# A hybrid trunk's mixer: large GpSimd operations moved to VectorE and ScalarE, and a chain's four output norms done at once

## The chip, the core and the metric

One core of a Trainium2 chip runs the whole program. The metric is the device time of one execution in microseconds; the value shown for a kernel is the median of its runs. Besides, one execution of each kernel is recorded by the hardware profiler. In its rows PE is TensorE (PEld its weight loads), DVE is VectorE, ACT is ScalarE, POOL is GpSimd and SP is SyncE, which issues the DMAs. L1124 is line 1124 of the kernel before.

## What is computed

A step of an encoder: 1024 prompt frames and 8 running streams of 16 frames (the "samples"), 1152 tokens of width 1024. A gated feed-forward (SwiGLU), a mixer, a second feed-forward, a final RMS norm. The mixer has two halves: four heads of a gated delta rule, and four groups of trailing means ("the pool half"). The delta rule of one head, cut from the reference:

```python
a_mat = jnp.where(strict, beta[..., :, None] * kk * decay, 0.0) + jnp.eye(chunk, dtype=f32)
sol = lax.linalg.triangular_solve(a_mat, rhs, left_side=True, lower=True, unit_diagonal=True)
u, w = sol[..., :dv], sol[..., dv:]
qk = jnp.einsum('bnhid,bnhjd->bnhij', q, k) * decay
def step(S, xs):
    q_c, qk_c, u_c, w_c, k_c, gl = xs
    v_new = u_c - jnp.einsum('bhcd,bhde->bhce', w_c, S)
    o_c = jnp.einsum('bhcd,bhde->bhce', q_c, S) + jnp.einsum('bhij,bhje->bhie', qk_c, v_new)
    S = S * jnp.exp(gl)[..., None, None] + jnp.einsum('bhcd,bhce->bhde', k_c, v_new)
    return S, o_c
...
o = rms_norm(o.astype(h.dtype), o_norm) * jax.nn.silu(gate.reshape(B, L, DN_HEADS, DN_HEAD_DIM))
```

Then the two halves are joined and multiplied with w_out. Everything is float32; the large products split each operand into a high and a low part and add three products.

## The kernel before

Tokens lie in the free dimension, channels in the partitions. The tokens come in three pieces: 512, 320 and 320. The program has three stages: the first feed-forward, the mixer, the second feed-forward. Only the mixer is touched.

The mixer runs over two blocks: block A has the first 512 tokens (four units of 128), block B has the other 512 prompt tokens and the 128 sample tokens. Per block and head there are tasks, written as Python generators: projections with a short convolution (letters p, v), the gate's projection (g), `prework` (w, and t for the samples), `inverse` (y and z), `chain` (c) or `chain_sample` (s), the pool half's means, mapping and split (m, n, x), and the product with w_out (o). The projections and the products with w_out, in a fixed list `fill`, are what keeps TensorE busy; the rest is urgent and small. A loop at the end writes the tasks into one program: it keeps a modelled time of TensorE, and where a generator yields a number it comes back to that task so many microseconds (times 1.35) later. The framework beneath then sets each engine's order from this program; an engine runs its own instructions strictly in that order. So an instruction that waits holds all that stands behind it on its engine.

What the change touches:

- `prework` computes decays, and from key products the matrix Vn (L1060), its pooled columns Vc (L1083, L1085), the query product AT (L1071). GpSimd scales the queries, q times U, in L1074, and raises a norm to a power in L1050.
- `inverse` solves the triangular system: GpSimd spreads Vc into Xs (L1096), TensorE multiplies it with a block matrix (the products of 384 columns, into `ps_b`), then fifteen small steps on VectorE (L1120, L1121), and L1124 places the blocks. GpSimd forms Gs, a masked Vn (L1131), for the merges that follow, which begin with transposes by TensorE (L62, into `ps_b`).
- `chain` steps through the four units of a head: a correction r, the new values vn (L1210), the new state (L1218), and the output `po`. `out_unit` norms it: ScalarE squares it with a sum (L1180) and copies it (L1181), VectorE scales the sum (L1182), GpSimd raises it to -1/2 (L1183), ScalarE multiplies (L1184). Its `finish` is a transpose by TensorE (L62, into `ps_c`) and VectorE's multiplication with the gate (L1190); it runs one unit later, for the last unit after a yield of 2.
- `chain_sample` does the same for the sample streams, each with a state of its own, S8: eight matrices of 128 columns. GpSimd masks vn eight times into `vz` (L1266) and scales S8 (L1268); two products of 512 columns are added to it by VectorE (L1275).
- `oz_split` splits a half's result into high and low for the product with w_out: ScalarE casts (L1008), and the low part is a subtraction (L1009) on GpSimd for the pool half, on VectorE for the other.

GpSimd also subtracts the low part of the weights of w_out (L186, 128x1024 each), and it copies small histories. VectorE evacuates the projections (L960, L963), runs the convolutions (L981, L987) and the pool half's means (L1323, L1329), and adds the outputs to x (L1002).

## Time and profile before

| | |
|---|---|
| median of 3 runs | 2192.55 us (2190.09 to 2193.48) |
| the profiled execution | 2195.53 us, its span 2193.7 us |
| TensorE busy | 2132.2 us, 97% of the span |
| VectorE, ScalarE, GpSimd busy | 1526.1, 917.5, 684.9 us |
| granted TensorE clock | 0.992 |
| chain of waits, by engine | PE 82%, DVE 10%, issue, DMA, POOL and ACT 2% each |

A row of a group of instructions reads: line, engine, operation, out<-in by the names of the buffers (their numbers left out), shape and count, then the busy time in microseconds, the mean of one in nanoseconds, and the idle time of the engine just before them with what ended it. A row of waits reads: who waited, for whom, microseconds in total, times, the longest. A row of the timeline: start, length, engine, line, operation, tiles, count, and in brackets the idle time before it. An idle engine off the bound costs nothing; what counts is where TensorE waits.

### The profile page before, as it was taken

Reading aid. Unit: us, or ns where it says so; the run is one execution under the profiler, and the core shown is the slowest. Engines: PE = TensorE matmul, PEld = TensorE weight load, DVE = VectorE, ACT = ScalarE, POOL = GpSimd, SP = SyncE. Lnnn points to the kernel's source line nnn. Section 1 sums busy time; section 2 is a strip of 40 time slices with the busy share of each in tenths; the row PEclk is TensorE's granted clock in tenths of the full one; section 3 lists DMA queues with packets and bytes.
Section 4 is the critical chain, followed back from the end, with each engine's and each line's share of the span. In section 5 each row is a group of like instructions: output and inputs, shape, how many; then the busy total and the mean of one; then the engine's idle time right before and its main releaser. Section 6 shows DMA issues by size and latency. Waiting matters only on the chain.

```text
span 2193.7 us, 33164 instructions
## 1 busy us (share of the span) xinstructions
PE 2132.2 (97%) x12341; PEld 1920.7 (88%) x12341; DVE 1526.1 (70%) x2736; ACT 917.5 (42%) x1854; POOL 684.9 (31%) x616
## 2 busy tenths in 40 slices
PE   9999999999999999999999998999999999999997
PEld 7899999998889887777989887889999999987997
DVE  7866666677347877778687867776666668743776
ACT  6433333444223455544444443543433335422333
POOL 1433333440014422322232333243333335100443
PEclk9999999999999999999999999999999999999998
DMA  6332333554556522111212123342333337446572
GB/s 252 120 124 103 128 109 112 183 202 147 184 195 218 179 86 61 57 61 59 94 55 80 44 93 93 134 145 92 127 110 123 115 129 248 142 125 225 198 256 74
DMA packets 102674, 289.72 MB, mean 132 GB/s; under 512 B 16240, under 2 KB 24304, under 8 KB 102256
## 3 DMA queue, kind: packets, MB, share of 16 engines
q1 hardware_dynamic: 101360, 286.40, 38.6%
q8 instruction: 97, 1.59, 0.3%
q10 hardware_dynamic: 1152, 1.19, 0.2%
q14 instruction: 65, 0.53, 0.1%
HBM read 214.89 MB, written 72.66 MB: 131 GB/s over the span
## 4 chain that ended last, share of the span: by engine, by line
PE 82%; DVE 10%; issue 2%; DMA 2%; POOL 2%; ACT 2%; DVEq 0%; SPq 0%; POOLq 0%; ACTq 0%
PE ps_a L58 31%; PE ps_b L58 20%; PE ps_d L58 17%; PE ps_c L58 14%; DVE O L288 2%; DVE B L981 1%; DVE O L186 1%; DVE A L1121 1%; PE ps_b L62 1%; DVE A L1323 1%; DMA x<-g_keep 1%; DVE x L654 1%; DMA R<-in_wd 1%; DVE A L1120 0%; POOL Q L282 0%
## 5 line engine op out<-in xcount | busy, mean ns | idle before, releaser
L58 PE MATMUL ps_a<-B,O 128*128 128x320 f32 x3040 | 509.1, 311 | 9.0 <-DVE x L654 5.8
L58 PEld LDWEIGHTS ps_a<-B,O 128*128 128x128 f32 x3040 | 465.7, 189 | 20.5 <-issue 8.6
L58 PE MATMUL ps_a<-A,O 128*128 128x320 f32 (+1 forms) x1952 | 426.3, 354 | 2.9 <-DVE A L1121 1.6
L58 PEld LDWEIGHTS ps_a<-A,O 128*128 128x128 f32 x1952 | 330.0, 190 | 37.6 <-issue 3.9
L288 DVE TENSOR_TENSOR O<-Q,O 128x512 fp32r<-128x512 f32 (+1 forms) x238 | 210.6, 886 | 193.6 <-ACT O L287 192.7
L58 PE MATMUL ps_b<-A,O 128*128 128x512 f32 (+1 forms) x1128 | 264.5, 388 | 5.2 <-ACT O L287 5.2
L58 PEld LDWEIGHTS ps_b<-A,O 128*128 128x128 f32 x1128 | 208.9, 189 | 45.8 <-ACT O L287 5.2
L58 PE MATMUL ps_d<-A,O 128*128 128x512 f32 x1056 | 244.2, 391 | 2.7 <-DVE x L606 1.8
L58 PEld LDWEIGHTS ps_d<-A,O 128*128 128x128 f32 x1056 | 196.8, 188 | 49.0 <-issue 4.0
L287 ACT CAST O<-Q 128x512 fp32r<-128x512 f32 (+1 forms) x238 | 143.2, 605 | 225.2 <-POOL Q L282 60.8
L288 DVE TENSOR_TENSOR O<-R,O 128x512 fp32r<-128x512 f32 (+1 forms) x216 | 197.7, 920 | 33.2 <-ACT O L287 32.4
L58 PE MATMUL ps_d<-B,O 128*128 128x320 f32 (+1 forms) x1104 | 206.1, 331 | 5.4 <-DVE x L1002 3.7
L282 POOL TENSOR_TENSOR Q<-R 128x512 f32<-128x512 f32 (+1 forms) x44 | 59.9, 1361 | 453.7 <-DMA R<-in_wd 279.0
L58 PE MATMUL ps_c<-A,O 128*128 128x512 f32 (+1 forms) x816 | 187.2, 377 | 0.8 <-DVE O L288 0.8
L58 PEld LDWEIGHTS ps_d<-B,O 128*128 128x128 f32 x1104 | 172.2, 189 | 16.1 <-DVE x L1002 5.9
L287 ACT CAST O<-R 128x512 fp32r<-128x512 f32 (+1 forms) x216 | 131.1, 611 | 126.5 <-PE ps_a L58 51.3
L58 PEld LDWEIGHTS ps_c<-A,O 128*128 128x128 f32 x816 | 145.6, 188 | 25.0 <-DVE O L288 1.3
L185 ACT CAST O<-R 128x1024 fp32r<-128x1024 f32 (+1 forms) x86 | 85.9, 1010 | 183.6 <-PE ps_d L58 133.7
L58 PE MATMUL ps_c<-B,O 128*128 128x320 f32 x912 | 144.6, 309 | 0.0
L58 PEld LDWEIGHTS ps_c<-B,O 128*128 128x128 f32 x912 | 136.8, 188 | 0.3
L393 POOL TENSOR_TENSOR A<-A,A 128x512 fp32r<-128x512 f32 x44 | 72.6, 1651 | 162.3 <-ACT A L392 162.2
L186 DVE TENSOR_TENSOR O<-R,O 128x1024 fp32r<-128x1024 f32 (+1 forms) x74 | 86.5, 1176 | 50.6 <-ACT O L185 29.7
(309 smaller groups left out, 3061.4 us busy)
## 6 DMA issues: line engine op xcount, KB each, us to landing
g_keep<-x SPq DMA_DIRECT2D x98, 320.0 KB, 2.5
R<-in_wg SPq DMA_DIRECT2D x48, 512.0 KB, 3.8
R<-in_wd SPq DMA_DIRECT2D x48, 512.0 KB, 3.7
R<-in_wu SPq DMA_DIRECT2D x47, 512.0 KB, 3.6
g_keep<-A SPq DMA_DIRECT2D x44, 512.0 KB, 2.6
A<-g_keep SPq DMA_DIRECT2D x44, 512.0 KB, 5.5
B<-g_keep SPq DMA_DIRECT2D x56, 320.0 KB, 6.3
A<-g_keep SPq DMA_DIRECT2D x42, 320.0 KB, 5.0
```

Of the source, the lines that this page charges most:

```text
L58: self.put(nc.tensor.matmul(out, lhs, rhs, **k), n / 2400 + .003 if lhs.dtype == F32R else max(n, lhs.shape[-1]) / 600)
L62: self.put(nc.tensor.transpose(out, lhs, rhs), out.shape[-1] / 1200)
L185: A.copy(hi, raw)
L186: (e or V).tensor_sub(lo, raw, hi.bitcast(F32))
L282: G.tensor_add(t, *src)
L287: Blocks.high = A.copy(hi, src).ins
L288: Blocks.mark = V.tensor_sub(lo, src, hi.bitcast(F32)).ins
L393: G.tensor_sub(go[:, 1], sg, go[:, 0].bitcast(F32))
L654: V.scalar_tensor_tensor(xk(c, d), ps, by, xk(c, d), ALU.mult, ALU.add)
L981: V.scalar_tensor_tensor(y[:, :512], raw[:, t:t + 512], cw[:, t:t + 1], y[:, :512], ALU.mult, ALU.add)
L1121: V.tensor_tensor(Uc[:, :, m + 1:], Uc[:, :, m + 1:], tu[:, :n, :w], ALU.add)
L1323: V.tensor_tensor(buf[:, :, :have], cur[:, :, w_:w_ + have], cur[:, :, :have], ALU.add)
```

## The change

The five larger GpSimd operations of `prework`, `inverse` and the pool half's split (L1074, both L1096, L1131, L1009 for the pool half) are issued on VectorE. In `chain_sample` the masked copies become eight ScalarE multiplications, and the scaling of S8 goes into VectorE's addition, which becomes eight operations that read one 128-column matrix, its scalar and the product in PSUM. `out_unit` is parted: `out_sums` squares and copies per unit, and `out_norm` does sum, power, four multiplications, four transposes into one PSUM tile and one multiplication with the gate, after the chain's last unit (yields 2.5 and 0.8, before 2 and 0.5). GpSimd keeps the powers and L186. The buffers for the sums hold four columns, the sample's output gets its own buffer, `osbs`.

```diff
--- before.py
+++ after.py
@@ -827,10 +827,10 @@
 
     ms.place(region("A4"), ("raw", WIDE, 2), ("ss", 32, 2), ("sss", 32, 2), ("ucar", 60, 1), ("cst", 288, 1))
     ms.place(region("A5"), ("Xs", 768, 1), ("DT", 512, 1), ("MV", 512, 1), ("DTs", P, 1), ("Vns", P, 1))
-    ms.place(region("A6"), ("z", WIDE, 1), ("Vc", 64, 1), ("Uc", 64, 1), ("tu", 64, 1), ("wpl", P, 1), ("sso", 1, 8), ("tt", 1, 8),
+    ms.place(region("A6"), ("z", WIDE, 1), ("Vc", 64, 1), ("Uc", 64, 1), ("tu", 64, 1), ("wpl", P, 1), ("sso", 4, 3), ("tt", 4, 3),
              ("half", 8, 1), ("small", 8, 1), ("nega", NH, 1), ("cout", 36, 1), ("Xss", 192, 1), ("Vc", 64, 1), ("vn", P, 2),
              ("sc", 120, 2), ("av", 80, 1), ("gm", 32, 1))
-    ms.place(region("R2"), ("eglS", 32, 1), ("scout", 288, 1), ("Vcs", 16, 2), ("Ucs", 16, 1), ("tus", 16, 1))
+    ms.place(region("R2"), ("eglS", 32, 1), ("osbs", P, 1), ("scout", 288, 1), ("Vcs", 16, 2), ("Ucs", 16, 1), ("tus", 16, 1))
     ms.place(region("R3"), ("big", 1024, 1))
     ms.place(region("B0"), ("k", 640, 1), ("q", 640, 1), ("gate", 640, 2))
     ms.place(region("B6"), ("k", 640, 1), ("q", 640, 1), ("kd", 512, 2), ("r", P, 1), ("rs", P, 1))
@@ -1071,7 +1071,7 @@
             V.tensor_tensor(AT, pqk, DT, ALU.mult)
 
             qv = q[:, c0:c0 + n * P].rearrange("p (u c) -> p u c", c=P)
-            G.tensor_tensor(qv, qv, U, ALU.mult)
+            V.tensor_tensor(qv, qv, U, ALU.mult)
             V.tensor_scalar(epsq, ssq, EPS, P * EPS, ALU.add, ALU.mult)
             yield 1.5
             pv = p3(n)
@@ -1093,7 +1093,7 @@
             e16 = cm[:, C_E16:C_E16 + 16]
             for m, lo, L in ((0, 0, 8), (8, 8, 8)):
                 w = 16 - lo
-                G.tensor_tensor(Xs[:, :, 16 * m:16 * m + L * w].rearrange("p u (m i) -> p u m i", m=L),
+                V.tensor_tensor(Xs[:, :, 16 * m:16 * m + L * w].rearrange("p u (m i) -> p u m i", m=L),
                                        Vc[:, :, lo:].unsqueeze(2).to_broadcast([P, n, L, w]),
                                        e16[:, m:m + L].unsqueeze(1).unsqueeze(3).to_broadcast([P, n, L, w]), ALU.mult)
             yield 1.3
@@ -1128,7 +1128,7 @@
                 yield 4
                 return
             Gs = mt("MV", 4, P)
-            G.tensor_tensor(Gs, Vn, cmat(C_M16).unsqueeze(1).to_broadcast([P, n, P]), ALU.mult)
+            V.tensor_tensor(Gs, Vn, cmat(C_M16).unsqueeze(1).to_broadcast([P, n, P]), ALU.mult)
             yield 8.5
             pT = p3(n)
             for u in range(n):
@@ -1173,26 +1173,30 @@
                             V.tensor_copy(dst, src)
             yield 0.8
 
-        def out_unit(h, pw, u, po, gate):
-
-            osb = mt("osb", P)
-            sso, t = mt("sso", 1), mt("tt", 1)
-            A.activation(osb, po, AF.Square, accum_out=sso)
+        def out_sums(pw, u, po, osb, sso):
+
+            A.activation(osb, po, AF.Square, accum_out=sso[:, u:u + 1])
             A.copy(osb, po)
-            V.scalar_tensor_tensor(t, sso, 1.0 / P, pw["epsq"][:, u:u + 1], ALU.mult, ALU.add)
-            G.tensor_tensor(t, t, half[:, 4:5], ALU.pow)
-            A.mul(osb, osb, t)
-
-            def finish():
-                po = pt("c")[:, :P]
-                T.transpose(po, osb, ident)
-                gv = gate[:, pw["c0"] + u * P:pw["c0"] + (u + 1) * P]
-                V.scalar_tensor_tensor(gv, gv, vec[:, 88:89], po, ALU.mult, ALU.mult)
-            return finish
+
+        def out_norm(pw, osb, sso, gate):
+
+            n = pw["n"]
+            t = mt("tt", 4)[:, :n]
+            V.scalar_tensor_tensor(t, sso, 1.0 / P, pw["epsq"], ALU.mult, ALU.add)
+            G.tensor_tensor(t, t, half[:, 4:4 + n], ALU.pow)
+            for u in range(n):
+                A.mul(osb[u], osb[u], t[:, u:u + 1])
+            yield 2.5
+            po = pt("c")[:, :n * P]
+            for u in range(n):
+                T.transpose(po[:, u * P:(u + 1) * P], osb[u], ident)
+            gv = gate[:, pw["c0"]:pw["c0"] + n * P]
+            V.scalar_tensor_tensor(gv, gv, vec[:, 88:89], po, ALU.mult, ALU.mult)
+            yield 0.8
 
         def chain(h, pw, gate):
             n = pw["n"]
-            done = []
+            osb, sso = [mt("osb", P) for _ in range(n)], mt("sso", 4)[:, :n]
             for u in range(n):
                 i = (pw["u0"] + u) * 4 + h
                 Sh = S[h]
@@ -1220,18 +1224,14 @@
                 if Sh is not None:
                     T.matmul(po, pw["qc"][u], Sh, start=True, stop=False)
                 T.matmul(po, pw["AT"][:, u], vn, start=Sh is None, stop=True)
-                done.append(out_unit(h, pw, u, po, gate))
-                if u:
-                    done.pop(0)()
+                out_sums(pw, u, po, osb[u], sso)
                 if Sh is not None:
                     free.append(Sh)
                 S[h] = Sn
                 yield 0.6
             if blk == 1:
                 SY.dma_start(pdelta[h], S[h])
-            yield 2
-            done.pop()()
-            yield 0.5
+            yield from out_norm(pw, osb, sso, gate)
 
         def chain_sample(h, pw, gate):
             i = 16 + h
@@ -1261,18 +1261,21 @@
             po = pt("c")[:, :P]
             T.matmul(po, okq[:, 1], ident, start=True, stop=False)
             T.matmul(po, pw["AT"][:, 0], vn, start=False, stop=True)
-            fin = out_unit(h, pw, 0, po, gate)
+            osb, sso = [mt("osbs", P)], mt("sso", 4)[:, :1]
+            out_sums(pw, 0, po, osb[0], sso)
+            fin = out_norm(pw, osb, sso, gate)
+            next(fin)
             vz = big.rearrange("p (b d) -> p b d", b=NB)
-            G.tensor_tensor(vz, vn.unsqueeze(1).to_broadcast([P, NB, P]),
-                            cm[:, C_IND:C_IND + 8].unsqueeze(2).to_broadcast([P, NB, P]), ALU.mult)
-            G.tensor_tensor(S8, S8, eglS[:, :, h].unsqueeze(2).to_broadcast([P, NB, P]), ALU.mult)
+            for b in range(NB):
+                A.mul(vz[:, b], vn, cm[:, C_IND + b:C_IND + b + 1])
             yield 3
-            fin()
+            next(fin)
             for j in range(2):
                 ps = pt("c")
                 T.matmul(ps, pw["kd"][:, 0], vz[:, 4 * j:4 * j + 4].rearrange("p b d -> p (b d)"), start=True, stop=True)
-                sv = S8[:, 4 * j:4 * j + 4].rearrange("p b d -> p (b d)")
-                V.tensor_add(sv, sv, ps)
+                for b in range(4 * j, 4 * j + 4):
+                    V.scalar_tensor_tensor(S8[:, b], S8[:, b], eglS[:, b, h:h + 1], ps[:, (b % 4) * P:(b % 4 + 1) * P],
+                                           ALU.mult, ALU.add)
                 yield 1.0
             SY.dma_start(sdelta[h], S8.rearrange("p b d -> p (b d)"))
 
@@ -1375,7 +1378,7 @@
                 mapped(NH - 1 - h, *mz[h])
                 yield 0.8
             if w == "x":
-                om[h] = oz_split(mz[h][0][:, :nt], mt("omh", 640), mt("oml", 640), G)
+                om[h] = oz_split(mz[h][0][:, :nt], mt("omh", 640), mt("oml", 640))
                 yield 1.5
             if w == "o":
                 oz = oz_split(gt[h][:, :nt])
```

The engines' orders move with it. In all orders below a row is a line, an operation, out<-in with the buffers' region and a running number, and a shape. VectorE at the first inverse of block A (B_666 holds Vn and U, A_660 takes Gs, the masked Vn and Xs one after the other, B_664 the queries, A_661 the pooled columns):

```order
+L1131 TENSOR_TENSOR A_660_6900<-B_666_6906,Q_6897 128x512
+L1074 TENSOR_TENSOR B_664_6904<-B_664_6904,B_666_6906 128x512
 L1083 TENSOR_TENSOR A_660_6900<-B_666_6906,Q_6897 128x512
+L1075 TENSOR_SCALAR A_659_6899<-A_659_6899 128x4
 L1085 TENSOR_REDUCE A_661_6901<-A_660_6900 128x64
-L1075 TENSOR_SCALAR A_659_6899<-A_659_6899 128x4
-L1292 TENSOR_TENSOR B_664_6904<-ps_a_7330,R_663_6903 128x512
+L1295 TENSOR_TENSOR B_664_6904<-ps_a_7330,R_663_6903 128x512
 L186 TENSOR_TENSOR O_725_7452<-R_723_7449,O_724_7451 128x1024
-L981 SCALAR_TENSOR_TENSOR B_667_6907<-A_659_6899,vec,B_667_6907 128x512
+L1096 TENSOR_TENSOR A_660_6900<-A_661_6901,Q_6897 128x4x128
+L1096 TENSOR_TENSOR A_660_6900<-A_661_6901,Q_6897 128x4x64
```

Two operations now stand in front of L1083, and Xs (L1096) behind the reduce, an evacuation and a weight split. TensorE at the same place (`ps_a` is a projection that fills it, `ps_b` of 384 columns the product with Xs), first where the two products stood, then where they stand:

```order
 L58 MATMUL ps_a_7364<-A_672_6923,O_714_7359 128x512
-L58 MATMUL ps_b_7276<-A_660_6900,Q_6897 128x384
 L58 MATMUL ps_a_7364<-A_670_6921,O_715_7360 128x512
-L58 MATMUL ps_b_7279<-A_660_6900,Q_6897 128x384
 L58 MATMUL ps_a_7364<-A_670_6921,O_714_7359 128x512
```
```order
 L58 MATMUL ps_a_7364<-A_671_6922,O_715_7360 128x512
 L58 MATMUL ps_a_7364<-A_671_6922,O_714_7359 128x512
+L58 MATMUL ps_b_7276<-A_660_6900,Q_6897 128x384
+L58 MATMUL ps_b_7279<-A_660_6900,Q_6897 128x384
 L58 MATMUL ps_a_7364<-A_673_6924,O_714_7359 128x512
```

Between the old and the new place of the first of them lie 14 products of the projection. TensorE at the end of the chain of head 2 in block A, before (the first row is the last unit's output product, L62 the transposes of the third and the fourth unit, `ps_d` products with w_out and a mapping):

```order
L58 MATMUL ps_c_8683<-A_661_6901,B_669_6909 128x128
L58 MATMUL ps_d_8736<-B_675_6960,A_661_6901 128x512
L62 MATMUL ps_c_8691<-ident,B_669_6909 128x128
L58 MATMUL ps_d_8739<-B_668_6908,O_887_8644 128x512 x2
L58 MATMUL ps_d_8739<-B_668_6908,O_888_8645 128x512
L58 MATMUL ps_d_8739<-B_668_6908,O_887_8644 128x512 x2
L58 MATMUL ps_d_8739<-B_668_6908,O_888_8645 128x512
L58 MATMUL ps_d_8753<-B_668_6908,O_902_8749 128x512 x2
L58 MATMUL ps_d_8753<-B_668_6908,O_903_8750 128x512
L58 MATMUL ps_d_8753<-B_668_6908,O_902_8749 128x512 x2
L58 MATMUL ps_d_8753<-B_668_6908,O_903_8750 128x512
L62 MATMUL ps_c_8761<-ident,B_669_6909 128x128
```

The same place now, up to the first unit's transpose; the other three stand six products further on:

```order
L58 MATMUL ps_c_8644<-A_661_6901,B_669_6909 128x128
L58 MATMUL ps_b_8652<-A_660_6900,Q_6897 128x384
L58 MATMUL ps_d_8697<-B_675_6960,A_661_6901 128x512
L58 MATMUL ps_d_8700<-B_668_6908,O_879_8605 128x512 x2
L58 MATMUL ps_d_8700<-B_668_6908,O_880_8606 128x512
L58 MATMUL ps_d_8700<-B_668_6908,O_879_8605 128x512 x2
L58 MATMUL ps_d_8700<-B_668_6908,O_880_8606 128x512
L62 MATMUL ps_c_8722<-ident,B_669_6909 128x128
```

Before, thirteen products stood between the last unit's output and its own transpose, and each earlier unit had the next unit's steps in between. Now eight stand between the last output and the first transpose, which waits for the norm of all four. At the same place in block B eleven products of 320 columns stand in between, at the last chain 24; at the other five ends more.

## The prediction

> **What bounds the kernel now.** I read the page first, then the busy time by stage, the waits of TensorE inside the mixer, and the stretches in which those waits lie.
>
> ```profile
> span 2193.7 us, 33164 instructions
> PE 2132.2 (97%) x12341; PEld 1920.7 (88%) x12341; DVE 1526.1 (70%) x2736; ACT 917.5 (42%) x1854; POOL 684.9 (31%) x616
> ```
>
> The table by stage has, in each row, the length of the stretch and then the busy time of PE, PEld, DVE, ACT and POOL. The rows are the first feed-forward, the mixer, the second feed-forward.
>
> ```profile
> 0.00:780.00 780.00, 768.85 (x4319) 698.71 (x4320) 533.25 (x770) 317.29 (x581) 250.50 (x194) 1.00 0.46 160
> 780.00:1400.00 620.00, 587.49 (x3625) 513.79 (x3624) 466.37 (x1200) 298.56 (x720) 174.46 (x227) 0.99 0.24 75
> 1400.00:2194.00 794.00, 775.86 (x4400) 708.25 (x4399) 526.50 (x767) 301.68 (x553) 259.98 (x195) 0.99 0.44 149
> ```
>
> TensorE is the bound, and the change touches the mixer alone and no matrix product of it. So all that it can win is the 620.0 - 587.5 = 32.5 us in which PE idles there. Who ends those waits:
>
> ```profile
> PE ps_c L62 <- ACT B L1184: 5.0, 4, 3.6
> PE ps_b L62 <- DVE B L1124: 4.7, 4, 2.0
> PE ps_d L58 <- DVE x L1002: 3.7, 4, 1.3
> PE ps_b L58 <- POOL A L1096: 2.7, 1, 2.7
> PE ps_c L62 <- DVE A L1120: 1.7, 1, 1.7
> PE ps_a L58 <- DVE A L1121: 1.6, 1, 1.6
> PE ps_d L58 <- POOL B L1009: 0.7, 1, 0.7
> ```
>
> Few name GpSimd, yet more hang on it. A stretch near the end of the mixer, and one VectorE operation in two homes:
>
> ```profile
> 1324.63 1.92 POOL L1268 TENSOR_TENSOR x<-x,R 128x1024 f32<-128x1024 f32 x1 [5.35 <-PE ps_c L58]
> 1324.76 4.69 DVE L1124 TENSOR_TENSOR B<-A,Q 128x128 f32<-128x128 f32 x4
> 1326.51 2.39 POOL L186 TENSOR_TENSOR O<-O,O 128x1024 fp32r<-128x1024 f32 x1
> ```
> ```profile
> L1124 DVE TENSOR_TENSOR B<-A,Q 128x128 f32<-128x128 f32 x32 | 15.5, 545 | 0.2
> L1124 DVE TENSOR_TENSOR x<-R,Q 128x128 f32<-128x128 f32 x4 | 1.1, 285 | 0.0
> L981 DVE SCALAR_TENSOR_TENSOR B<-A,vec,B 128x512 f32<-128x512 f32 x66 | 57.9, 877 | 8.5 <-ACT B L979 8.2
> L981 DVE SCALAR_TENSOR_TENSOR x<-A,vec,x 128x512 f32<-128x512 f32 x6 | 4.5, 745 | 0.0
> L1182 DVE SCALAR_TENSOR_TENSOR A<-A,A 128x1 f32<-128x1 f32 x36 | 12.9, 358 | 3.0 <-ACT B L1180 2.8
> ```
>
> Four operations of 0.285 us (L1124) take 4.69 us while two GpSimd operations run: VectorE, reading two operands from SBUF, stands still until GpSimd is done. In the means this is 32 x (545 - 285) ns = 8.3 us at L1124 and 66 x (877 - 745) ns = 8.7 us at L981. Both are VectorE time that GpSimd costs today.
>
> **The change part by part.** *The first inverse (L1131, L1074, L1096).* GpSimd does Gs, q times U and Xs in a row:
>
> ```profile
> 833.81 1.28 POOL L1131 TENSOR_TENSOR A<-B,Q 128x512 f32<-128x512 f32 x1 [4.78 <-DVE B L1060]
> 835.05 1.75 POOL L1074 TENSOR_TENSOR B<-B,B 128x512 f32<-128x512 f32 x1
> 836.82 2.66 POOL L1096 TENSOR_TENSOR A<-A,Q 128x512 f32<-128x512 f32 x2
> 839.54 1.57 PE L58 MATMUL ps_b<-A,Q 128*128 128x384 f32 x2 [2.70 <-POOL A L1096]
> ```
>
> VectorE's prices for the moved shapes, and the pace of PE (start, length, count: 24 products of 512 columns, 101 of 320):
>
> ```profile
> L1323 DVE TENSOR_TENSOR A<-A 128x512 f32<-128x512 f32 x2 | 1.4, 686 | 0.0
> L1323 DVE TENSOR_TENSOR A<-A 128x240 f32<-128x240 f32 x4 | 1.6, 399 | 0.0
> L1190 DVE SCALAR_TENSOR_TENSOR B<-B,vec,ps_c 128x128 f32<-128x128 f32 x31 | 10.6, 340 | 5.3 <-PE ps_c L62 5.2
> L1009 DVE TENSOR_TENSOR B<-x,B 128x640 fp32r<-128x640 f32 x1 | 0.8, 818 | 0.0
> L186 DVE TENSOR_TENSOR O<-O,O 128x1024 fp32r<-128x1024 f32 x14 | 17.1, 1218 | 2.2 <-ACT O L185 2.0
> L1085 DVE TENSOR_REDUCE A<-A 128x64 f32<-128x512 f32 x8 | 8.3, 1038 | 0.1
> ```
> ```profile
> 1060.60 14.82 PE ps_a L58 x101
> 1398.16 5.44 PE ps_a L58 x24
> ```
>
> From 833.81 on, VectorE's new queue (the order in the part on the change) holds the end of L1071 (0.5), four operations of 512 columns (4 x 0.69 = 2.7), a small one (0.2), the reduce (1.04), the weight split (1.22) and Xs (0.69 + 0.40): 6.8 us, so Xs is ready at 840.6, a microsecond later than today. But PE reaches the product later too: it now stands behind 14 more products of 5.44/24 = 0.227 us, so at 839.54 - 2.70 + 3.18 = 840.0. The wait falls from 2.7 to 0.6: -2.1 us.
>
> *The waits behind held VectorE operations (L1124).* In the stretch above L1268 goes, and the four L1124 would run before L186 begins. At the other three waits also a GpSimd operation that goes (L1268, and twice L1009) lies just ahead. I take 3.7 of the 4.7 us.
>
> *The output norm.* 36 powers of one column on GpSimd become 12, and the norm of a chain comes once. Today:
>
> ```profile
> 1131.74 2.18 POOL L1266 TENSOR_TENSOR R<-B,Q 128x1024 f32<-128x1024 f32 x1
> 1135.93 2.20 POOL L1183 TENSOR_TENSOR A<-A 128x1 f32<-128x1 f32 x1 [1.63 <-DVE A L1182]
> 1138.62 0.33 PE L62 MATMUL ps_c<-ident,B 128*128 128x128 f32 x1 [3.60 <-ACT B L1184]
> ```
> ```profile
> 1366.95 0.39 PE L58 MATMUL ps_c<-A,B 128*128 128x128 f32 x2
> 1370.10 0.33 PE L62 MATMUL ps_c<-ident,B 128*128 128x128 f32 x1 [0.32 <-ACT B L1184]
> ```
> ```profile
> L1184 ACT ACTIVATE B<-B,A 128x128 f32<-128x128 f32 x36 | 14.5, 402 | 41.9 <-POOL A L1183 39.1 <-POOL A L972 2.6
> ```
>
> The transposes' waits (L1184 5.0, and 1.7 at L1120) end with the per-unit norms. In their place stand eight chain ends. From a unit's last product to its transpose takes 1370.10 - 1366.95 = 3.15 us; with three more scalings of 0.402 before the last unit it is 4.35. By the new PE order the first transposes of a chain have 5.6 us or more of other products in front of them at five of the eight ends (no wait), 24 x 14.82/101 = 3.5 us at the last chain (none or 0.1), but only one product of 384 and seven of 512 columns, 1.9 us, at head 2 of block A, and eleven of 320, 1.6 us, at head 2 of block B. There PE waits 1.2 + 1.5 = 2.7 us. So -6.7 + 2.7 = -4.0 us. ScalarE, behind which other casts are queued, loses two thirds of its 39.1 us of standing for the power; that covers the 32 scalings of the sample state, 12.9 us, that it gains below.
>
> *The pool half's split (L1009).* 1.5 us on GpSimd becomes 0.69 or 0.82 on VectorE; the 0.7 us wait at the end goes.
>
> *The sample state.* L1266 (2.0 us each) becomes eight ScalarE scalings, 8 x 0.402 = 3.2 us per head; the first product needs only four (1.6 us), as soon as today. L1268 goes; the two additions of 512 columns (0.69 us) become eight of 128 that read PSUM (0.340 by the row of L1190): 2.7 instead of 1.4 us. [...] The two DMAs of the state, and SyncE's queue, only trade places with neighbours.
>
> *VectorE's bill.* Added: 8 prework tasks x (0.69 + 0.69 + 0.69 + 0.40) = 19.8 us, the four samples' 4 x (0.285 + 0.285 + 0.2) = 3.1, eight splits 4 x 0.69 + 4 x 0.82 = 6.0, the state 4 x 1.3 = 5.3; saved: 24 of 36 sums (L1182) at 0.358, 8.6, and 28 of 36 gate products, 36 x 0.34 against 8 x 0.69 + 4 x 0.34, 5.4. Net +20.2. Given back by GpSimd: of the 17.0 us at L1124 and L981 I take half, 8.5, since the splits of L186 stay on GpSimd. That leaves 12 us more on 466 in 620. VectorE ends PE waits only where it is late, some 12 us in the list for 466 busy; in that ratio 12 us cost 0.3. I take +1.0. Bounds: -8 (all the held time returns) to +12 (all of it on the path).
>
> Sum: -2.1 - 3.7 - 4.0 - 0.7 + 1.0 = -9.5 us. The profiled execution took 2195.53 us, its span 2193.7; it lies 3.0 above the median of the runs, 2192.55. 2195.5 - 9.5 = 2186.0, so 2183.0 for the median.
>
> **The rivals.** *VectorE becomes the bound (slower).* Xs, Gs and q times U stand in its queue in front of the inverse's chain of small operations. If the held time doesn't return, 20 us are added; if half of that falls on PE's waits and the first inverse gains nothing, the sum is +10 - 3.7 - 4.0 - 0.7 = +1.6, and with all 20 it is +11.6: 2194 to 2204. It decides from 13 of the 20 us on, where the sum passes +4.4. For it: these operations stand ahead of the inverse in order. Against it: VectorE is busy 466 of 620 us, 75%.
>
> *The chain's end (slower).* Four scalings in a row on ScalarE behind a weight cast of a microsecond, at all eight ends: 8 x (1.2 + 1.0) = 17.6 instead of 2.7. That makes the sum +5.4, 2198. For it: the queue is in order. Against it: five ends have 5.6 us of cover.
>
> *GpSimd's small operations are locked out in turn (smaller gain).* The power that took 2.20 us ran beside VectorE's pooling, which reads two operands:
>
> ```profile
> 1136.85 0.88 DVE L1329 SCALAR_TENSOR_TENSOR A<-A,A 128x512 f32<-128x512 f32 x2
> ```
> ```profile
> L1183 POOL TENSOR_TENSOR A<-A 128x1 f32<-128x1 f32 x36 | 22.8, 635 | 70.5 <-DVE A L1182 69.8
> ```
>
> The mean of all 36 is 0.635. The more VectorE reads two operands, the more often a power is held. At the three thin ends that is 3 x 1.6 = +4.7: sum -4.8, 2187.8. [...]
>
> *Only the places move (no change).* PE's order is different from the first inverse on; waits of 32.5 us may reappear elsewhere: 2192.5 within 4.
>
> **How the numbers follow.** A measurement here can tell about 0.2%, 4.4 us, from no change. My forecast 0.56; the lock-out 0.12, of which 0.07 is still faster and 0.05 the same; waits only moved 0.15; VectorE 0.10; the chain's end 0.07. Faster 0.56 + 0.07 = 0.63, same 0.15 + 0.05 = 0.20, slower 0.17. The best case ends every wait in the list but L1002's: -17.0 us, 2175.5. The range goes from a little below that, 2174, to 2196, into both slower cases; the likeliest case's own range is 2175 to 2188.
>
> **What would show it.** Right: PE idle in the mixer near 23 us; L1124 near 0.3 us; no PE wait on Xs over 1 us; transposes' waits at head 2 of both blocks; VectorE near 475 us there. Wrong: VectorE over 490 us in the mixer, PE waits behind it grown, or waits of 2 us and more at most chain ends.

## The result and the profile after

The changed kernel takes 2174.80 us (median of 5 runs, 2172.10 to 2176.37), the kernel before on the same chip 2193.22 (2190.09 to 2193.95): ratio 0.9914, 95% interval 0.9901 to 0.9928, or -18.4 us where -9.5 was forecast. The profiled execution took 2173.01 us.

The page's span and busy times, and the table by stage (length, then busy PE, PEld, DVE, ACT, POOL; granted clock, DMA share, GB/s) of the changed kernel:

```profile
span 2171.2 us, 33111 instructions
...
PE 2121.9 (98%) x12341; PEld 1914.9 (88%) x12341; DVE 1525.1 (70%) x2764; ACT 924.8 (43%) x1886; POOL 607.1 (28%) x532
```
```profile
0.00:780.00 780.00, 767.82 (x4317) 697.94 (x4318) 534.56 (x770) 317.25 (x581) 250.40 (x194) 1.00 0.47 160
780.00:1380.00 600.00, 580.86 (x3633) 511.31 (x3632) 462.40 (x1229) 306.78 (x754) 96.92 (x143) 1.00 0.25 78
1380.00:2171.00 791.00, 773.17 (x4395) 705.61 (x4393) 528.12 (x767) 300.74 (x553) 259.74 (x195) 0.99 0.44 150
```

The mixer holds the gain: it ends some 20 us earlier. PE idles 19.1 us in its 600 where 32.5 stood in 620. Two columns are to be read together: PE's idle time, and the clock, 0.99 before and 1.00 now. One per cent of 620 us is 6 us. The row was quoted in the prediction, and the column wasn't read.

TensorE's waits in the mixer after (total us, times, longest):

```profile
PE ps_d L58 <- DVE x L1002: 4.0, 5, 1.1
PE ps_a L58 <- DVE O L186: 2.1, 1, 2.1
...
PE ps_b L62 <- DVE B L1124: 1.1, 2, 0.9
...
PE ps_a L58 <- ACT O L185: 0.9, 1, 0.9
...
PE ps_c L62 <- ACT B L1188: 0.6, 1, 0.6
```

L1096 (2.7) and L1184 (5.0) are gone and L1124 is down from 4.7. New is L185, the cast of a weight, and the wait for its split (L186) has grown from 0.5 to 2.1. VectorE's operations whose means told of the hold (VectorE standing still while GpSimd works):

```profile
L981 DVE SCALAR_TENSOR_TENSOR B<-A,vec,B 128x512 f32<-128x512 f32 x66 | 51.6, 782 | 3.4 <-ACT B L979 3.1
L1124 DVE TENSOR_TENSOR B<-A,Q 128x128 f32<-128x128 f32 x32 | 7.1, 284 | 0.2
```

L1124 went from a mean of 545 to 284 ns, its unheld price; L981 from 877 to 782, with 745 unheld.

**The clock.** The kernel before around its wait of 2.70 us for Xs (stretch, length, busy times, clock, DMA share, GB/s):

```profile
836.00:839.00 3.00, 0.84 (x4) 0.36 (x2) 2.89 (x4) 1.75 (x5) 2.98 (x3) 1.00 0.00 0
839.00:840.00 1.00, 0.46 (x1) 0.42 (x2) 0.00 (x0) 0.00 (x0) 0.48 (x1) 0.83 0.30 16
840.00:843.00 3.00, 3.00 (x6) 1.69 (x5) 0.66 (x1) 1.25 (x3) 0.00 (x0) 0.50 0.51 169
```

After the wait TensorE works at half clock. The clock's own record has one stretch of 3.413 us here, 839.65 to 843.06; it costs half, 1.7 us, and appears as busy time. The wait cost 2.7 + 1.7 = 4.4 us. The mixer before has four such stretches, at 805.52, 839.65, 1140.03 and 1375.55; after it has one, at 906.34. So idle time and clock together give -13.3 - 3 x 1.7 = -18.4 us. That this is the measured difference of the medians to the tenth is luck: the two traced executions lie 22.5 us apart (2195.53 and 2173.01), and 4 us of that are in neither count.

Whether a wait does this is chance in part. The same wait for L1124, 1.96 us, ended at 1329.10 in the kernel before and at 1329.12 in the first experiment below. First the kernel before, then that experiment:

```profile
1330.00:1333.00 3.00, 3.00 (x24) 3.00 (x24) 0.48 (x1) 1.43 (x4) 1.55 (x1) 1.00 0.00 0
```
```profile
1330.00:1333.00 3.00, 3.00 (x13) 3.00 (x13) 0.00 (x0) 1.42 (x3) 1.54 (x1) 0.50 0.00 0
```

In the same 3 us 24 products run in the one and 13 in the other. Within one kernel's trace all stretches begin on one grid of 3.413 us: those at 839.65 and 1140.03 lie 88.0 lengths apart. In these two traces the wait counted by how it fell on that grid. In the kernel before a border of the grid, at 1327.8, parts this wait, and the length behind the border has 1.34 us of idle time; in the experiment one length, 1326.25 to 1329.66, has 2.51 us. The mixers of the 14 traces have 28 stretches, two of them two lengths long. In the 3.41 us ahead of them PE had idled 1.1 to 2.9 us. Each of the 22 lengths with 1.93 us or more of idle time was followed by one; of those with 1.1 to 1.9 us six were, and most were not. So in these traces 1.1 to 2.9 us of idle time in one length could be enough.

### The profile page after: what moved, and what is told of

Read it like the earlier page. It is cut to its first block, busy times and chain, and to the rows that moved or that the text cites. A ratio compares the mean times of both kernels' runs of the same rounds, so it can differ in the third digit from the quotient of the medians.

```text
span 2171.2 us, 33111 instructions
## 1 busy us (share of the span) xinstructions
PE 2121.9 (98%) x12341; PEld 1914.9 (88%) x12341; DVE 1525.1 (70%) x2764; ACT 924.8 (43%) x1886; POOL 607.1 (28%) x532
## 4 chain that ended last, share of the span: by engine, by line
PE 80%; DVE 10%; DMA 4%; issue 2%; ACT 2%; POOL 2%; SPq 0%; DVEq 0%; POOLq 0%; ACTq 0%
PE ps_a L58 29%; PE ps_b L58 19%; PE ps_d L58 17%; PE ps_c L58 14%; DVE O L288 2%; DMA R<-in_wd 1%; DVE x L654 1%; DMA B<-g_keep 1%; POOL Q L282 1%; DMA O<-in_wd 1%; PE ps_b L62 1%; DVE A L1120 1%; DVE A L1121 1%; ACT O L287 1%; DMA x<-g_keep 1%
## 5 line engine op out<-in xcount | busy, mean ns | idle before, releaser
L185 ACT CAST O<-R 128x1024 fp32r<-128x1024 f32 (+1 forms) x86 | 85.9, 1010 | 183.7 <-PE ps_d L58 134.7
L186 DVE TENSOR_TENSOR O<-R,O 128x1024 fp32r<-128x1024 f32 (+1 forms) x74 | 87.2, 1185 | 50.5 <-ACT O L185 29.8
## 6 DMA issues: line engine op xcount, KB each, us to landing
R<-in_wg SPq DMA_DIRECT2D x48, 512.0 KB, 3.8
R<-in_wd SPq DMA_DIRECT2D x48, 512.0 KB, 3.7
R<-in_wu SPq DMA_DIRECT2D x47, 512.0 KB, 3.6
g_keep<-A SPq DMA_DIRECT2D x44, 512.0 KB, 2.7
A<-g_keep SPq DMA_DIRECT2D x44, 512.0 KB, 5.5
```

Source lines behind the costliest of these rows:

```text
L185: A.copy(hi, raw)
L186: (e or V).tensor_sub(lo, raw, hi.bitcast(F32))
```

## The experiments

Ratios are to the kernel before in the same session (medians 2190.4 to 2193.2 us), from 4 to 12 runs each; the column "us" is the ratio less one, times that median. The columns from "held" on are counted in the trace of one execution, from 780 us to the power at the mixer's end (L232): *held*, by how much VectorE's operations that overlap a GpSimd operation exceed the shortest of their line and shape (where it is more than 60 ns); *work*, the rest of the sum of VectorE's durations (which overlap a little, so that the sum exceeds the busy time of the views: before, 529.9 us against 466.4); *idle*, PE's idle time; *half*, lengths of 3.413 us at half clock. What a hold looks like, in the kernel before at 1324.76: two L1124, begun 0.13 and 0.11 us after L1268 and L186, took 1.94 and 2.42 us and ended 0.15 us after them; the two that followed took 0.28 each.

| kernel | ratio (95%) | us | held | work | idle | half |
|---|---|---|---|---|---|---|
| before | 1 | 0 | 47.3 | 482.6 | 32.0 | 4 |
| changed | 0.9914 (0.9901-0.9928) | -18.9 | 20.2 | 509.6 | 18.7 | 1 |
| norm alone | 0.9998 (0.9988-1.0007) | -0.4 | 38.5 | 476.6 | 30.3 | 5 |
| prework alone | 0.9961 (0.9949-0.9973) | -8.5 | 37.9 | 507.4 | 24.9 | 2 |
| state and split alone | 0.9960 (0.9948-0.9972) | -8.8 | 33.0 | 494.2 | 25.2 | 2 |
| changed + unread products | 1.0081 (1.0068-1.0094) | +17.7 | 47.8 | 508.0 | 42.2 | 6 |
| changed + weight split | 0.9865 (0.9849-0.9881) | -29.6 | 0.7 | 528.7 | 10.6 | 1 |
| changed + unread copies | 0.9980 (0.9971-0.9988) | -4.4 | 32.5 | 512.0 | 28.4 | 4 |
| changed without norm | 0.9912 (0.9898-0.9926) | -19.3 | 24.9 | 517.4 | 17.8 | 0 |
| the same + weight split | 0.9860 (0.9840-0.9879) | -30.7 | 1.0 | 540.1 | 9.5 | 0 |
| state alone | 0.9965 (0.9954-0.9977) | -7.7 | 36.1 | 489.5 | 26.2 | 0 |
| pool half's split alone | 0.9985 (0.9975-0.9995) | -3.3 | 42.6 | 492.2 | 28.5 | 2 |
| changed + weight split + unread | 0.9952 (0.9940-0.9965) | -10.5 | 23.8 | 529.9 | 23.5 | 1 |
| weight split alone | 0.9944 (0.9932-0.9956) | -12.3 | 25.1 | 502.9 | 20.3 | 2 |

The change of idle, plus 1.7 us for each change of half, gives every measured difference within 5 us, eight of thirteen within 3 (unread copies: 28.4 - 32.0 = -3.6, measured -4.4). It can't be closer: idle and half come from one execution, the ratio from several. For the state alone, whose traced execution was the fastest of its five, it gives -12.6 where -7.7 was measured.

**1. Norm alone.**

```diff
-        def out_unit(h, pw, u, po, gate):
+        def out_sums(pw, u, po, osb, sso):
+        def out_norm(pw, osb, sso, gate):
...
-            G.tensor_tensor(t, t, half[:, 4:5], ALU.pow)
+            G.tensor_tensor(t, t, half[:, 4:4 + n], ALU.pow)
```

> The kernel before with the output norm of a chain done at once, and nothing else. Theory of the hold (a GpSimd operation of two SBUF operands keeps VectorE standing, 28 us less of it in the mixer after, and the norm is worth only its own waits): the transposes' waits go (L1184 5.0 and L1120 1.7 us), the hold stays near 50 us, so -4.0 to -6.7 us, ratio 0.997 to 0.998. Rival, the norm did most of it (the chains' ends are the path, the rest only moves places): -13 to -18 us, ratio 0.992 to 0.994.

Measured: nothing, below both expectations. Two of its longest waits, and a stretch of block A:

```profile
PE ps_a L58 <- DVE O L186: 2.1, 1, 2.1
PE ps_c L62 <- ACT R L1188: 2.0, 1, 2.0
```
```profile
908.23 0.63 ACT L989 ACTIVATE B<-B 128x512 f32<-128x512 f32 x1 [4.61 <-DVE B L981]
...
908.76 1.03 ACT L185 CAST O<-R 128x1024 fp32r<-128x1024 f32 x1
...
909.85 0.73 PE L58 MATMUL ps_a<-A,O 128*128 128x512 f32 x2 [0.97 <-ACT O L185]
...
912.66 1.61 PE L58 MATMUL ps_a<-A,O 128*128 128x512 f32 x4 [2.08 <-DVE O L186]
```

The transposes' waits fall from 6.7 us to 2.6, now at L1188: 2.0 of them, the row with R, are a sample's, whose norm has one unit before and after, and 0.6 a chain's. TensorE, stopped less, comes sooner to the products of the next weight. Its cast L185 stands on ScalarE behind L989, which waits 4.61 us for VectorE's convolution; the split L186 follows. PE waits 0.97 + 2.08 there, and at 913.24 a half-clock stretch begins. So 0 is the sum of a gain, of new waits and of one more length at half clock.

**2. Prework alone.**

```diff
-            G.tensor_tensor(qv, qv, U, ALU.mult)
+            V.tensor_tensor(qv, qv, U, ALU.mult)
...
-                G.tensor_tensor(Xs[:, :, 16 * m:16 * m + L * w].rearrange("p u (m i) -> p u m i", m=L),
+                V.tensor_tensor(Xs[:, :, 16 * m:16 * m + L * w].rearrange("p u (m i) -> p u m i", m=L),
...
-            G.tensor_tensor(Gs, Vn, cmat(C_M16).unsqueeze(1).to_broadcast([P, n, P]), ALU.mult)
+            V.tensor_tensor(Gs, Vn, cmat(C_M16).unsqueeze(1).to_broadcast([P, n, P]), ALU.mult)
```

> The kernel before with Gs, q times U and Xs (L1131, L1074, L1096) on VectorE, and nothing else. Theory of the hold: the first inverse's wait of 2.7 us goes (-2.1 or more), and 6.8 us of hold at these three lines comes back to VectorE, at a third of a microsecond of TensorE each (what was left of the 18.4 us after the first inverse and the norm's 6.7, over 28 us): -2.1 - 2.3 = -4.4 us, ratio 0.998. Rival, VectorE's bill: 20 us of added operations ahead of the inverse's chain cost more than they give: 0 to +5 us, ratio 1.000 to 1.002. Rival, the norm did most of it: within 2 us of before.

Measured: -8.5 us, twice the expectation; VectorE's bill as a loss is out. The waits:

```profile
PE ps_b L62 <- DVE B L1124: 4.6, 4, 2.0
...
PE ps_c L62 <- ACT B L1184: 1.6, 3, 0.8
```

Not only L1096 is gone: the transposes' wait fell from 5.0 to 1.6 us with the norm per unit as before, and two of four half-clock stretches went.

**3. State and split alone.**

```diff
-            G.tensor_tensor(vz, vn.unsqueeze(1).to_broadcast([P, NB, P]),
-                            cm[:, C_IND:C_IND + 8].unsqueeze(2).to_broadcast([P, NB, P]), ALU.mult)
-            G.tensor_tensor(S8, S8, eglS[:, :, h].unsqueeze(2).to_broadcast([P, NB, P]), ALU.mult)
+            for b in range(NB):
+                A.mul(vz[:, b], vn, cm[:, C_IND + b:C_IND + b + 1])
...
-                om[h] = oz_split(mz[h][0][:, :nt], mt("omh", 640), mt("oml", 640), G)
+                om[h] = oz_split(mz[h][0][:, :nt], mt("omh", 640), mt("oml", 640))
```

> The kernel before with the sample state's scaling and masking off GpSimd (L1266, L1268) and the pool half's split (L1009) on VectorE, and nothing else. Theory of the hold: 5.9 + 4.7 + 5.5 = 16 us of held VectorE time come back, at a third each -5.4 us, and L1124's and L1009's waits are among them: -5 to -6 us, ratio 0.997 to 0.9975. Rival, the norm did most of it or VectorE's bill eats it (eight operations of 128 columns in the place of two of 512): within 2 us of before, ratio 0.999 to 1.001.

Measured: -8.8 us, more than the 5 to 6 expected. L1124 has left the head of the list, while the waits that hang on the prework and the norm stay:

```profile
PE ps_c L62 <- ACT B L1184: 3.2, 4, 1.6
...
PE ps_b L58 <- POOL A L1096: 2.7, 1, 2.7
```

The three parts alone (1, 2 and 3) add up to -17.7 of the -18.9 us.

**4. Unread products.** Results that nobody reads, to put the hold back without a producer in the path:

```diff
+            for _ in range(4):
+                G.tensor_tensor(mt("dummy", 4, P), Vn, cmat(C_M16).unsqueeze(1).to_broadcast([P, n, P]), ALU.mult)
...
+            for b in (0, 4, 0, 4):
+                G.tensor_tensor(mt("dummy", 4, P), vn.unsqueeze(1).to_broadcast([P, 4, P]),
+                                cm[:, C_IND + b:C_IND + b + 4].unsqueeze(2).to_broadcast([P, 4, P]), ALU.mult)
...
+                G.tensor_sub(mt("dummy", 512), mz[h][0][:, :512], om[h][0][:, :512].bitcast(F32))
```

> The changed kernel, to which GpSimd gets operations back whose results nobody reads: four products of 512 columns at each of the four heads of both blocks where Gs is made, four for each sample state and one for each pool half's split, 56 in all, two SBUF operands each, near 1.3 us each or 73 us of GpSimd. No operation of the kernel waits for one of them, except those queued behind them on GpSimd. Theory of the hold: VectorE's held time in the mixer grows from 22 to 45 us or more and the time by a third of that, +8 us, ratio to the changed kernel 1.0035. Rival, the cost was that GpSimd stood as producer in the path: within 2 us of the changed kernel, though the held time grows.

Measured: 37 us slower than the changed kernel, more than four times the expectation; GpSimd as producer alone is out. GpSimd's unread groups, and the waits:

```profile
L1133 POOL TENSOR_TENSOR R<-B,Q 128x512 f32<-128x512 f32 x32 | 47.1, 1472 | 24.8 <-DVE B L1060 23.0
...
L1274 POOL TENSOR_TENSOR R<-B,Q 128x512 f32<-128x512 f32 x16 | 20.3, 1266 | 6.3 <-DVE B L1261 3.9 <-DVE A L1113 1.5
...
L1387 POOL TENSOR_TENSOR R<-A,B 128x512 f32<-128x512 f32 x6 | 10.5, 1743 | 9.6 <-ACT B L1008 6.4 <-issue 3.1
```
```profile
PE ps_b L58 <- DVE A L1096: 3.9, 1, 3.9
...
PE ps_c L62 <- ACT B L1190: 3.4, 1, 3.4
PE ps_c L62 <- ACT R L1190: 3.2, 2, 2.2
```

These rows and two more splits (3.4 us) are 81.3 us of GpSimd. They bring back 27.6 of hold, 23.5 of PE's idle time and five half-clock stretches. L1190 is ScalarE's scaling behind the norm's power (L1188 of the changed kernel), which here stands in GpSimd's queue behind the unread work. So the result mixes two costs: hold, and the queue.

**5. Unread copies.** The same places, one operand each:

```diff
+            for _ in range(7):
+                G.tensor_copy(mt("dummy", 4, P), Vn)
...
+            for _ in range(6):
+                G.tensor_copy(mt("dummy", 4, P), vn.unsqueeze(1).to_broadcast([P, 4, P]))
...
+                for _ in range(2):
+                    G.tensor_copy(mt("dummy", 512), mz[h][0][:, :512])
```

> The changed kernel with unread GpSimd operations at the same places as in the run with unread products, but copies of one operand, more of them (7 of 512 columns per head and block, 6 per sample state, 2 per split), so that GpSimd works about as long. Theory of the hold (what costs is VectorE standing while GpSimd reads two operands): hold stays near 23 us, within 3 us of the changed kernel. Rival (what cost 33 us there was GpSimd's queue, behind which the norm's powers and the weight splits stood): most of it is there again, +15 us or more, ratio to before 1.000 or more.

Measured: 14 us slower than the changed kernel, so neither theory as stated.

```profile
PE ps_b L62 <- DVE B L1124: 2.6, 4, 1.1
...
PE ps_c L62 <- ACT B L1190: 1.9, 1, 1.9
...
PE ps_c L62 <- ACT R L1190: 1.4, 1, 1.4
```

The copies took nearly as long as the products (73.8 us against 81.3), but VectorE was held 12.3 us more, not 27.6: a copy holds too, but less. The products, with 15.3 us more of hold, cost 22 us more. Not all of that need be the hold: GpSimd works 7.5 us longer there, and the waits at L1190 are 6.6 us against 3.3. Of the copies' own 14 us, L1190 with GpSimd's queue is 3.3 us by name; what hold and queue share of the rest stays open.

**6. Weight split on VectorE too.**

```diff
-            return load_unit(src, None, G if kind in "o" else V)
+            return load_unit(src, None, V)
```

> The changed kernel with the split of the output weights (L186, 16 of 1024 columns in the mixer) on VectorE too. After the change it is the last GpSimd operation that holds VectorE there (19.6 of 23.3 us). Theory of the hold: a held microsecond counts like a busy one, 19.6 us go and 16 x 1.22 = 19.5 us of VectorE come, the waits stay: within 3 us of the changed kernel, ratio to before 0.990 to 0.993. Rival, GpSimd's hold is worse than work, because it falls in the midst of the chains' small operations: 5 us or more faster than the changed kernel, ratio 0.989 or less. Rival, VectorE is at its limit: 4 us or more slower, ratio 0.993 to 0.996.

Measured: 0.9865, 11 us faster than the changed kernel, and with 8 the fastest here; the even exchange is wrong. VectorE's operations are at their unheld prices:

```profile
L981 DVE SCALAR_TENSOR_TENSOR B<-A,vec,B 128x512 f32<-128x512 f32 x66 | 49.2, 746 | 1.1 <-ACT B L979 0.7
L186 DVE TENSOR_TENSOR O<-R,O 128x1024 fp32r<-128x1024 f32 x38 | 46.4, 1220 | 4.6 <-ACT O L185 2.7 <-PE ps_a L58 1.3 <-issue 0.3
```

The longest wait left is a new one, for a transfer: the pool weights, 2.2 us.

**7. Changed without the norm** (experiments 2 and 3 together).

> The kernel before with the prework's, the sample state's and the split's operations off GpSimd (the second and third part run alone, together); the output norm stays per unit. Theory, time is TensorE's idle time plus 1.7 us for each stretch of 3.4 us at half clock, and the two parts end different waits: -8.4 - 8.2 = -16.6 us, ratio 0.992, and so within 3 us of the changed kernel. Rival, the norm is worth nothing alone but 4 us or more with the others: slower than the changed kernel by that, ratio 0.9935 or more. Rival, the norm at once costs (its new wait at the split of a weight, 0.9 + 2.1 + 1.7 us after the change): faster than the changed kernel by 3 us or more, ratio 0.990 or less.

Measured: 0.9912, the changed kernel's 0.9914. The norm at once is worth nothing beside the others either:

```profile
PE ps_c L62 <- DVE A L1120: 1.9, 2, 1.7
...
PE ps_c L62 <- ACT B L1184: 0.7, 2, 0.4
```

Without it the transposes wait 0.7 us for the norm's scaling, and the wait at L1120 that hid the late weight stands again.

**8. The same with the weight split on VectorE** (7 with the edit of 6).

> The run before this one (no norm at once), with the split of the output weights on VectorE as well. Theory of the hold: within 3 us of that run, as VectorE's 19.5 us of work take the place of as much hold. If the hold is worse than work: faster than all the others, ratio 0.988 or less; if VectorE is at its limit: slower than that run by 4 us or more, since it has 24 small sums and 28 gate products more than the changed kernel (14 us).

Measured: 0.9860, as fast as 6 with 11 us more VectorE work: VectorE's busy time is not the bound.

**9. and 10. State alone, pool half's split alone** (the two diffs of 3, apart).

> The kernel before with the sample state's masking on ScalarE and its scaling merged into the addition (L1266, L1268), nothing else: four heads, 16 us of GpSimd, 10.6 us of hold. Theory of the hold (near 1.2 us of time for each held microsecond, as the unread copies and products gave; 20 us of busy time on VectorE or ScalarE cost half as much): most of the 8.2 us of both parts, -5 to -9 us, ratio 0.996 to 0.998. Rival, GpSimd's own waits count (TensorE waits for the split by name, L1009 0.7 us, and never for the state): within 2 us of before.

> The kernel before with the pool half's split (L1009) on VectorE, nothing else: eight operations, 5.5 us of hold go and 6 us of VectorE come. Theory of the hold: -2 to -5 us, ratio 0.998 to 0.999. Rival, work for hold is an even exchange: -0.7 to +1 us, ratio 1.000.

Measured: -7.7 and -3.3 us. No wait of TensorE before names the state's two operations, and alone they are worth nearly as much as the prework (-8.5). With the state alone L1124's mean is down a third:

```profile
L1124 DVE TENSOR_TENSOR B<-A,Q 128x128 f32<-128x128 f32 x32 | 10.0, 375 | 0.2
```

The even exchange is just excluded for the split.

**11. Weight split on VectorE, hold put back.** Edit 6, and unread subtractions at its place:

```diff
+        for c in hold:
+            G.tensor_sub(mt("dummy", 512), raw[:, c:c + 512], hi[:, c:c + 512].bitcast(F32))
```

> The changed kernel with the output weights' split on VectorE (the run that was the fastest so far), and on GpSimd at the same place two unread subtractions of 512 columns of the same operands, 32 in all and some 40 us in the mixer, as long as the split there was. VectorE then has the work and the hold. Theory of the hold: the gain over the changed kernel (10 us and more) goes and VectorE's 19.5 us of work stay, so 5 to 15 us slower than the changed kernel, ratio to before 0.994 to 0.999. Rival, the gain came because the split is ready 1.2 us sooner on VectorE (1.22 us against 2.4): the gain stays, ratio 0.986 to 0.988.

Measured: 0.9952, 8 us slower than the changed kernel; an earlier split was not the gain of 6. The unread groups:

```profile
L188 POOL TENSOR_TENSOR R<-R,O 128x512 f32<-128x512 f32 x24 | 42.0, 1751 | 42.7 <-issue 28.8 <-ACT O L185 12.8
L188 POOL TENSOR_TENSOR R<-O,O 128x512 f32<-128x512 f32 x8 | 15.6, 1945 | 22.5 <-ACT O L185 17.0 <-issue 4.6 <-POOL R L990 0.5
```

TensorE's waits, first in 6, then here (the added lines move every later line by two, so L1002, L1188 and L1222 are L1004, L1190 and L1224):

```profile
PE ps_c L62 <- ACT B L1188: 1.9, 2, 1.3
...
PE ps_d L58 <- DVE x L1002: 0.3, 1, 0.3
PE ps_c L58 <- DVE B L1222: 0.3, 1, 0.3
```
```profile
PE ps_d L58 <- DVE x L1004: 2.8, 4, 1.2
PE ps_c L58 <- DVE B L1224: 2.2, 2, 1.4
...
PE ps_c L62 <- ACT B L1190: 1.1, 2, 0.6
```

Against 6, 23.1 us of hold at equal work cost 19 us, 0.8 each. GpSimd's queue comes back with the hold, and no run parts the two. But what returns by name is waiting behind VectorE, while the wait for the norm's scaling, which hangs on a power in that queue, is shorter than in 6; new besides is 1.5 us at the weight's cast (L185). Against the changed kernel, 20.3 us of work and 3.6 of hold cost 8.3, so a microsecond of work some 0.3 (8.3 - 3.6 x 0.8 = 5.4, over 20.3; 0.1 to 0.5 by the intervals). The two prices are those of these runs and no rule. For the norm alone (8.8 us less hold, 6.0 less work) they give -9 us, and -0.4 was measured; for the prework alone (9.4 less hold, 24.8 more work) they give 0, and -8.5 was measured. So a held microsecond has no fixed cost.

**12. Weight split alone, on the kernel before.**

> The kernel before with the output weights' split on VectorE, and none of the parts of the change: GpSimd keeps the prework, the state, the pool half and the norms. 23.0 us of hold go and 19.5 us of VectorE come. Theory of the hold: as on the changed kernel, 10 to 13 us faster than before, ratio 0.994 to 0.9955. Rival, the last holds count and the first don't (waits end only when nothing holds VectorE any more): within 3 us of before.

Measured: 0.9944, -12.3 us, inside the expectation. One line gives two thirds of the whole change's gain. The waits that the change ended stand at the head of its list:

```profile
PE ps_c L62 <- ACT B L1184: 3.1, 3, 2.0
PE ps_b L62 <- DVE B L1124: 2.9, 3, 1.5
PE ps_b L58 <- POOL A L1096: 2.7, 1, 2.7
```

## Why the prediction was right in direction and half in size

**The first inverse, -2.1: right.** PE does not wait for Xs; the product starts at 838.74, where the prediction had 840.0 with 0.6 of wait. Xs is ready at 838.60, not 840.6; 1.3 us of that is that VectorE comes to this place sooner (L1060 at 831.29, before 832.60). The half-clock stretch behind the old wait, 1.7 us, was not in the sum.

```profile
837.58 1.02 DVE L1096 TENSOR_TENSOR A<-A,Q 128x512 f32<-128x512 f32 x2
...
838.74 1.53 PE L58 MATMUL ps_b<-A,Q 128*128 128x384 f32 x4
```

**L1124, -3.7: right.** 4.7 became 1.1; the mean 284 ns was forecast as 0.3 us.

**The output norm, -4.0: wrong.** "The transposes' waits (L1184 5.0, and 1.7 at L1120) end with the per-unit norms" was the step that failed. Experiments 1 and 7 measure 0. The longest L1184 wait, 3.6 of the 5.0 us (the row at 1138.62 in the prediction), is a sample's. Its norm has one unit before and after, so the norm at once can't end it; in experiment 1, 2.0 us of it stay. What made its power late are two holds. GpSimd stood idle for 1.63 us until VectorE had made the sum (L1182), and VectorE was behind because a product of one column (L1049) had taken 1.85 us while L1266 ran; the power itself then took 2.20. In the kernel before:

```profile
1131.33 0.15 DVE L1049 TENSOR_TENSOR A<-A,A 128x4 f32<-128x4 f32 x1
...
1132.08 1.85 DVE L1049 TENSOR_TENSOR A<-A,A 128x1 f32<-128x1 f32 x1
...
1135.70 0.15 DVE L1182 SCALAR_TENSOR_TENSOR A<-A,A 128x1 f32<-128x1 f32 x1
```

Most of the L1184 wait goes with the prework alone (5.0 to 1.6), and 0.7 is left once prework, state and split are off GpSimd. The L1120 wait does end with the norm, but it had covered the late cast of the next weight: 0.91 + 2.07 + 1.7 us of half clock appear there after. That cast is late by a hold too, that of the weight split which the change leaves on GpSimd. In the changed kernel VectorE's L1120 takes 2.33 us beside it (0.19 without), and the convolution that ScalarE waits for stands behind:

```profile
896.81 2.39 POOL L186 TENSOR_TENSOR O<-O,O 128x1024 fp32r<-128x1024 f32 x1
896.92 2.33 DVE L1120 TENSOR_TENSOR A<-A,A 128x28 f32<-128x28 f32 x1
```

The feared waits at head 2 (2.7) are 0.6.

**The pool half's split, -0.7: too small.** Alone it is worth -3.3 (interval -1.1 to -5.5), more than its own wait. The rest fits the hold at L1009: with it gone L1184's wait falls from 5.0 to 3.6 us and L1124's from 4.7 to 2.9. No run parts that hold from the rest of the edit.

**VectorE's bill, +1.0: the term that was mis-sized.** The prediction gave half of 17.0 us of hold back, from two lines' means; over all lines 27.1 went (47.3 to 20.2), as much as the work that came (27.0). So VectorE is as busy as before: the pages have 1526.1 us before and 1525.1 after, 1520.7 with edit 6 and 1522.9 with edit 12 alone. At nearly one busy time the kernel runs at 0, -19, -30 and -12 us. So "in that ratio 12 us cost 0.3" had the wrong unit: held and worked microseconds are no like coin. In experiment 11 a held one costs 0.8 and a worked one 0.3. That a hold is worse because it stops a chain's small operation for as long as 2.4 us, while added work waits in places of its own, is argued and not shown.

**The clock: not in the sum.** Three half-clock stretches fewer are -5.1 us of the 8.9 that the forecast missed. The other 3.8 are idle time, 13.3 us less where 9.5 was forecast: more than forecast from the parts that take hold away, less from the norm.

**The range: held by luck.** 2174.8 lies below the prediction's best case (2175.5) and below its likeliest case's own range, and only 0.8 us inside the stated one. The low end was meant for every listed wait ending; in fact fewer went, and the clock, which no term counted, made up for them. Two of its sums are off besides: the listed waits without L1002's are 16.4 us, not 17.0, and if all 17.0 us of held time return, its own terms leave 20.2 - 17.0 = 3.2 us of added work, no gain of 8.

**The rivals.** VectorE as the bound is refuted by 8 (11 us more work, no slower). The chain's end: no such waits. GpSimd's small operations locked out: the norm's powers do take 0.54 to 2.14 us, and 3 of 12 lie 0.49 to 1.5 us above the shortest of their size, each of them beside VectorE operations of two SBUF operands (before, 5 of 36 by 0.35 to 1.66 us), but ScalarE's 8.7 us of waiting for them reach PE in 0.6 only. That places only move was right for one part, the norm. The idle time promised (23) came out at 19.1, VectorE in the mixer (475) at 462 in a stretch 20 us shorter.

## What to carry to other kernels

Price a GpSimd operation of two SBUF operands by what VectorE can't do meanwhile (in the mixer before it was held for 47.3 us, L1124 at a mean of 545 ns against 284), even if no wait names it: compare the means of one VectorE operation in a place with GpSimd and in one without, over all its lines. Read the granted clock beside the idle time, since here the TensorE wait of 2.70 us for Xs cost 1.7 more that appeared as busy time. Where a wait goes, look for what it hid, and try the parts alone; here the largest edit did nothing, and one line that the change left out was worth most.

## What the runs showed of the hardware beyond that

- In the mixers half clock came in lengths of 3.413 us on a fixed grid, and a wait of 1.96 us got one in one trace and none in another. Time and clock scattered together between executions of one kernel: in the 12 runs with the pool half's split alone, mean clocks of 0.997 went with 2182.7 and 2183.1 us, 0.993 with 2191.7 and 2192.5.
- A GpSimd copy of 512 columns (0.73 to 0.82 us), with one operand read, held VectorE as well: with 96 copies VectorE was held 12.3 us more, and 11.2 us of hold lie on operations that overlap such copies alone.
